# A two-layer hybrid encoder: layer 0 projects x before its norm is known

## The chip, the cores and the metric

The kernel runs on one core of a Trainium2 chip. The core has a matrix engine (TensorE, PE in the profile, with its weight loads as PEld), a vector engine (VectorE, DVE), a scalar engine (ScalarE, ACT), a general engine (GpSimd, POOL) and SyncE (SP), which here only issues loads. The metric is the device time of one execution in microseconds (us).

## What is computed

Two layers over 256 tokens of width 2048, all in float32. A layer norms its input, projects it to seven groups of columns, runs a convolution group and an attention group, joins them in an output projection, and adds a normed embedding times a gate. The reference, cut to what matters:

```python
for i in range(DEPTH):                      # DEPTH = 2
    hn = _rmsnorm(h, norm_g[i])
    u = hn @ w_in[i]
    a_val, a_glu, a_z, q, k, v, b_z = jnp.split(u, offs, axis=-1)
    ya = _conformer_conv(a_val, a_glu, ...) * jax.nn.silu(a_z)
    yb = _window_attention(q, k, v, bias_band, sink[i]) * jax.nn.silu(b_z)
    h = h + jnp.concatenate([ya, yb], axis=-1) @ w_out[i]
    e = _rmsnorm(p[i] @ w_pe[i], pe_g[i])
    h = h + e * jax.nn.sigmoid(h @ w_pg[i])
return _rmsnorm(h, final_g)
```

`_rmsnorm(x, g)` is x times g, divided by the root of the mean square of the token's 2048 values.

## The kernel before

Everything is kept transposed: channels lie on the 128 partitions, the 256 tokens along the row. A float32 product is made of three fast ones (`mm3`, lines 398 to 403): weights and operand are each split into a rounded part and the rest (hi and lo), and hi x hi, hi x lo and lo x hi are summed in a PSUM bank.

Weights come as a stream of half tiles of 128 x 1024 values, two to a load of 1 MB (`load`, line 158, into one of three `raw` buffers, issued by SP). `split` (line 163) makes hi on ACT (a cast) and lo on DVE (a subtraction) into one of five `w` buffers; `ahead` and `get` keep it four halves ahead of use. One half tile feeds 24 matmuls, a step. After each step `pump` (line 203) issues some taps of the convolution on DVE (`conv`, line 557, 3.3, 2.6 or 3.3 taps a step by stage) and one piece of each side generator (`embed`, `attention`, `lnorm`). For PE, DVE and ACT the order of the program is the order of execution; the DMA queues run theirs in order too.

The order of a layer: embedding e = p @ w_pe (eight pairs of tiles), convolution tiles `ag` (value and gate, 8), k, v, then pairs of zb and q with the attention behind them, za, the output projection o in two halves (first the attention's part, then the convolution's), and the gate g.

Layer 0 starts so: loads of p, the first weights and x on two queues (lines 281 to 296). The embedding's matmuls run in plain float32, since its weights needn't be split then. Meanwhile ACT squares x, DVE sums the squares into `hacc`, and PE sums over the partitions (`rstd_col`, line 349); POOL takes the power -0.5, PE transposes the root into a row (`rstd_row`, line 364). Only then `operand` (line 447) makes x times gain times root, split into `hg`, and the `ag` matmuls start. The first two `ag` tiles run together (line 584). `glu` (line 573) evicts a tile: ACT takes the sigmoid of the gate from PSUM into `u`, DVE multiplies it with the value into `a` (a part of the tile az).

`embed` (line 521) issues the squares of e between the convolution's steps: ACT squares, POOL adds into `eacc`; later come the root and the scaling of e. `bias_prep` (line 326) makes the attention's bias by one matmul `fps`. In the attention, q is evicted into `qq` (line 691): for each half ACT scales it, DVE makes the rest; the scores `sc` (line 636) follow two steps later.

## Time and profile before

| what | us |
|---|---|
| median of 3 runs | 937.8 |
| lowest of them | 936.86 |
| the profiled execution | 938.7 |
| its span, from first to last instruction | 936.9 |

The mean granted clock of PE was 0.996. In the profile a row of the timeline reads: start, duration, engine, line of the code, operation, what it writes and reads, shape, count, and in brackets how long the engine was idle before it and what ended that. A row of the windows reads: the stretch, its length, then busy time and count for PE, PEld, DVE, ACT and POOL (only those that a filter leaves), the granted clock, the busy share of the DMA engines and GB/s. A row of groups ends in count, total and mean ns of one.

### The profile page before, as it was taken

The numbers are of one execution on the slowest core, as the hardware profiler recorded it, in microseconds if no ns is written. First come the engines' busy times: TensorE is split into PE (matmuls) and PEld (weight loads), VectorE is DVE, ScalarE is ACT, GpSimd is POOL, SyncE is SP. The second block draws the span as 40 slices with busy tenths as digits, with TensorE's granted clock in tenths as the row PEclk, the third lists the DMA queues.
The fourth block names the chain that finished last, engine by engine and source line by source line (L and its number), as shares of the span: only waits on it lengthen the run. The fifth ranks groups of instructions, "written<-read, shape, count | busy, mean of one in ns | idle before, by whom it ended". The sixth has DMA issues, their size and how long they took to land.

```text
span 936.9 us, 19106 instructions
## 1 busy us (share of the span) xinstructions
PE 923.9 (99%) x7960; PEld 909.7 (97%) x7960; DVE 767.6 (82%) x1282; ACT 549.2 (59%) x830; POOL 82.0 (9%) x79
## 2 busy tenths in 40 slices
PE   8999999999999999999999999999999999999995
PEld 7999999999999999999999999999999999999995
DVE  3999999998887786787679999999888877777663
ACT  4655454878874555554566445568788546445551
POOL 0013001001000000011102100100100000000111
PEclk9999999999999999999999999999999999999999
DMA  7674656555547455546555556565555554654532
GB/s 298 226 250 150 220 180 230 190 196 175 189 171 247 166 209 212 191 181 230 211 189 193 181 212 226 174 213 196 183 169 180 193 197 152 247 183 179 200 114 91
DMA packets 29011, 182.55 MB, mean 195 GB/s; under 512 B 3595, under 2 KB 4156, under 8 KB 9084
## 3 DMA queue, kind: packets, MB, share of 16 engines
q1 hardware_dynamic: 24284, 165.70, 50.1%
q0 software_dynamic: 3344, 12.88, 4.2%
q10 hardware_dynamic: 1296, 2.75, 0.8%
q8 instruction: 62, 1.02, 0.4%
q14 instruction: 25, 0.20, 0.1%
HBM read 177.09 MB, written 4.23 MB: 194 GB/s over the span
## 4 chain that ended last, share of the span: by engine, by line
PE 75%; DVE 19%; ACT 2%; issue 2%; DMA 1%; ACTq 0%; DVEq 0%
DVE cz L566 8%; DVE w L171 8%; PE o L401 6%; PE o L402 6%; PE o L403 6%; PE g L401 6%; PE g L403 6%; PE g L402 6%; PE ag L403 4%; PE ag L401 4%; PE ag L402 4%; PE za L401 3%; PE za L403 3%; PE za L402 3%; PE av L679 2%
## 5 line engine op out<-in xcount | busy, mean ns | idle before, releaser
L171 DVE TENSOR_TENSOR w<-raw,w 128x1024 fp32r<-128x1024 f32 x306 | 375.1, 1234 | 99.5 <-ACT w L168 98.6
L168 ACT CAST w<-raw 128x1024 fp32r<-128x1024 f32 x308 | 315.6, 1046 | 157.8 <-PE ag L403 42.5
L566 DVE SCALAR_TENSOR_TENSOR cz<-az,pars,cz 128x241 f32<-128x241 f32 (+11 forms) x480 | 215.9, 499 | 1.0
L401 PE MATMUL ag<-hg,w 128*128 128x256 f32 x512 | 141.8, 277 | 0.0
L403 PE MATMUL ag<-hg,w 128*128 128x256 f32 x512 | 141.6, 277 | 0.0
L402 PE MATMUL ag<-hg,w 128*128 128x256 f32 x512 | 141.5, 276 | 0.0
L403 PE MATMUL g<-h,w 128*128 128x256 f32 x512 | 141.3, 276 | 0.0
L401 PE MATMUL g<-h,w 128*128 128x256 f32 x512 | 141.3, 276 | 0.0
L402 PE MATMUL g<-h,w 128*128 128x256 f32 x512 | 141.3, 276 | 0.0
L401 PEld LDWEIGHTS ag<-hg,w 128*128 128x128 f32 x512 | 96.1, 188 | 0.9 <-ACT u L575 0.8
L403 PEld LDWEIGHTS ag<-hg,w 128*128 128x128 f32 x512 | 96.2, 188 | 0.1
L402 PEld LDWEIGHTS ag<-hg,w 128*128 128x128 f32 x512 | 96.1, 188 | 0.0
L401 PEld LDWEIGHTS g<-h,w 128*128 128x128 f32 x512 | 96.1, 188 | 0.0
L402 PEld LDWEIGHTS g<-h,w 128*128 128x128 f32 x512 | 96.1, 188 | 0.0
L403 PEld LDWEIGHTS g<-h,w 128*128 128x128 f32 x512 | 96.1, 188 | 0.0
L401 PE MATMUL za<-hg,w 128*128 128x256 f32 x256 | 71.7, 280 | 0.0
L401 PE MATMUL o<-yb,w 128*128 128x256 f32 x256 | 71.6, 280 | 0.0
L401 PE MATMUL q<-hg,w 128*128 128x256 f32 x256 | 71.5, 279 | 0.0
L401 PE MATMUL zb<-hg,w 128*128 128x256 f32 x256 | 71.5, 279 | 0.0
L402 PE MATMUL o<-yb,w 128*128 128x256 f32 x256 | 71.0, 277 | 0.0
L402 PE MATMUL q<-hg,w 128*128 128x256 f32 x256 | 71.0, 277 | 0.0
L403 PE MATMUL zb<-hg,w 128*128 128x256 f32 x256 | 71.0, 277 | 0.0
(223 smaller groups left out, 2264.4 us busy)
## 6 DMA issues: line engine op xcount, KB each, us to landing
raw<-in_wst SPq DMA_DIRECT2D x153, 1024.0 KB, 4.9
bias<-fscr POOLq DMA_DIRECT2D x16, 384.0 KB, 3.9
raw<-in_wst SPq DMA_DIRECT2D x4, 512.0 KB, 7.9
az<-in_xT POOLq DMA_DIRECT2D x4, 512.0 KB, 6.0
hscr<-e POOLq DMA_DIRECT2D x2, 1024.0 KB, 5.6
az<-hscr POOLq DMA_DIRECT2D x4, 512.0 KB, 5.4
x<-in_xT SPq DMA_DIRECT2D x3, 512.0 KB, 8.2
out_t<-og ACTq DMA_DIRECT2D x4, 256.0 KB, 3.0
```

The source lines that it names most:

```text
L168: nc.scalar.copy(hi, raw)
L171: nc.vector.tensor_sub(lo, raw, hi.bitcast(F32))
L401: nc.tensor.matmul(o, w[:, 0], x[:, 0], start=start, stop=False, skip_group_check=True)
L402: nc.tensor.matmul(o, w[:, 0], x[:, 1], start=False, stop=False, skip_group_check=True)
L403: nc.tensor.matmul(o, w[:, 1], x[:, 0], start=False, stop=stop, skip_group_check=True)
L566: nc.vector.scalar_tensor_tensor(acc[:, t, lo_:hi_], a[:, t, lo_ + s:hi_ + s], w(k), acc[:, t, lo_:hi_], ALU.mult, ALU.add)
L679: nc.tensor.matmul(o[hh * HD:(hh + 1) * HD, x, :], v[:, kt, g * HD:(g + 1) * HD], pt[hh][:, kt, :], start=x == 0 and kt == 0, stop=kt == 1 ...
```

## The change

In layer 0 the operand is x times gain alone, so that no matmul of the projection waits for the norm; the root multiplies the results. As the factor belongs to a token, which lies along the row, DVE multiplies each result by a row of roots (`evicted`), and v, with tokens on partitions, is scaled by a column in ACT's copy. The root is taken from a second copy of x with tokens on partitions (`xtok`): ACT squares eight pieces and accumulates each piece's sum, DVE adds them, POOL takes the power, PE transposes.

The first two `ag` tiles are loaded in pieces and multiplied in four groups of four k-slices each, as the pieces land. The embedding of layer 0 comes behind them, in three products. x by tokens, p and the constants are loaded later. In both layers the squares of e move to the second half of the output projection, with DVE in place of POOL for the sums, and the root's row there gets two more small matmuls (`settle`). Layer 0 issues 3.2 taps a step in the first stage, and one warming matmul is added.

```diff
-NWARM = 6
-QQ = ((4, 5), (2, 4))
+NWARM = 7
+QQ = (2, 4)
...
-    for q in range(4):
-        out.append(("w_pe", q, 0, 2))
+    if l:
+        out += W_PE
     for ts in FIRST_TILES:
         for k0 in (0, 8):
             for t in ts:
                 for off in (OFF_VAL, OFF_GLU):
                     out.append(("w_in", off + tile_cols(t), k0, 8))
+        if l == 0 and len(ts) == 2:
+            out += W_PE
...
+        raw = raws[h // 2][:, h % 2, c] if h // 2 in raws else alone[h][:, c]
+        hi, lo = spl[h][:, 0, c], spl[h][:, 1, c]
         nc.scalar.copy(hi, raw)
-        spl[h] = w
-        if h not in (4, 5):
-            nc.vector.tensor_sub(lo, raw, hi.bitcast(F32))
-    def first_lo(h):
-        w = spl[h]
-        nc.vector.tensor_sub(w[:, 1], raws[h // 2][:, h % 2, :], w[:, 0].bitcast(F32))
+        nc.vector.tensor_sub(lo, raw, hi.bitcast(F32))
...
-    RATES = (3.3, 2.6, 3.3)
+    RATES = ((3.2, 2.6, 3.3), (3.3, 2.6, 3.3))
...
-    load_half(0, 0, nc.scalar, 2)
-    pf = load_p(0)
-    load_half(0, 1)
-    load_x(0, nc.scalar)
...
+    load_x(0, 1)
+    load_part(0, 0, nc.scalar, 4)
+    nc.sync.dma_start(gains, gain)
+    load_x(1, 1)
+    load_part(0, 1, nc.scalar, 4)
+    load_x(2, 2)
+    load_part(1, 0, nc.scalar)
+    load_part(2, 0, nc.scalar)
+    load_part(3, 0)
     load_x(4)
-    load_half(1, 0, nc.scalar)
+    for x in range(4):
+        load_part(x, 1)
     load_x(8)
+    for x in range(4, 8):
+        load_part(x, 0)
     load_x(12)
-    load_half(1, 1)
-    load_half(2, 0)
-    nc.sync.dma_start(gains, gain)
-    load_half(2, 1)
+    for x in range(4, 8):
+        load_part(x, 1)
...
+    def small_loads():
+        for t in (pf[:, 0, 0:1], xts[0][:, 0:1]):
+            nc.vector.memset(t, 0.0)
+        nc.sync.dma_start(pf, pT[0])
+        for x, y in enumerate(xts):
+            nc.sync.dma_start(y, xtok[x // 4, :, x % 4 * 2 * S:(x % 4 + 1) * 2 * S])
+    def later_loads():
+        for t in (pars[:, 0:1], oh[:, 0:1], sinkt[:, 0:1]):
+            nc.vector.memset(t, 0.0)
+        nc.sync.dma_start(pars, par)
...
-                if l == 0 and j // 2 < 4:
-                    for k in (4 * (j // 2), 4 * (j // 2) + 2):
-                        if k < KT - 2:
-                            square_acc(hacc, h[k // 8][:, k % 8:k % 8 + 2, :], k == 0, nc.vector)
-                    if j // 2 == 3:
-                        sq = wk.tile([P, 2, S], F32, name="sq", tag="sq", bufs=3)
-                        nc.scalar.activation(sq, h[1][:, 6:8, :], AF.Square)
-                        hparts = halves_of(sq) + [fold(hacc)]
-                if j // 2 == QQ[l][0]:
-                    dg = rstd_col(hparts, D, f"rh{l}")
-                    ahead(5 if l == 0 else Cursor.h - 1 - q + 5)
-                if j // 2 == QQ[l][1]:
-                    rbs.append(rstd_row(dg, f"rh{l}", copy=False))
-                    if l == 0:
-                        first_lo(4)
-                        operands(0, 1)
-                        first_lo(5)
-                        subs.pop(0)()
-                        operands(2, 1)
...
+            for n in range(4):
+                c = slice((n % 2) * (HALF // 2), (n % 2 + 1) * (HALF // 2))
+                ks = range(4 * n, 4 * n + 4)
+                for y in range(4):
+                    for k in ks[2 * y:2 * y + 2]:
+                        i, kk = k // 8, k % 8
+                        hi, lo = (x[:, kk, :] for x in halves(hg[i]))
+                        nc.scalar.activation(hi, h[i][:, kk, :], AF.Copy, scale=gcol(l, k))
+                        nc.vector.scalar_tensor_tensor(lo, h[i][:, kk, :], gcol(l, k), hi.bitcast(F32),
+                                                       ALU.mult, ALU.subtract)
+                    if n == 0 and y == 0:
+                        split_part(0, slice(0, HALF // 4))
+                        split_part(0, slice(HALF // 4, HALF // 2))
+                    else:
+                        split_part(4 * (n // 2) + y, c)
+                if n == 1:
+                    small_loads()
+                for y in range(4):
+                    w = spl[4 * (n // 2) + y].rearrange("p t (k c) -> p t k c", k=8)
+                    for k in ks:
+                        mm3(firsts[y // 2][:, y % 2, :], w[:, :, k % 8, :], hg[k // 8][:, :, k % 8, :],
+                            y % 2 == 0 and k == 0, k == KT - 1)
+            for y in range(8):
+                spl.pop(y)
+            Cursor.h = 8
+            pp = wk.tile([P, 4 * S + 32], F32R, name="pp", tag="qq")
+            pp = pp[:, 24:24 + 4 * S].rearrange("p (x k s) -> p x k s", x=2, k=2)
+            hilo(pp[:, 0], pp[:, 1], pf)
+            ahead(8)
+            later_loads()
+            xs = wk.tile([P, 2, 4], F32, name="xs", tag="xs", bufs=1)
+            for x, y in enumerate(xts):
+                nc.scalar.activation(y, y, AF.Square, accum_out=xs[:, x // 4, x % 4:x % 4 + 1])
+            nc.vector.tensor_add(xs[:, :, 0:2], xs[:, :, 0:2], xs[:, :, 2:4])
+            nc.vector.tensor_add(xs[:, :, 0], xs[:, :, 0], xs[:, :, 1])
+            rcol = root(xs[:, :, 0], D, f"rh{l}")
+            ahead(9)
+            scaled = rstd_row(rcol, f"rh{l}", settle=2)
...
+        def evicted(b, scale=None, scaled=scaled):
+            if scaled is None:
+                return b
+            u = wk.tile([P, 2, S], F32, name="ev", tag="sq", bufs=3)
+            if scale is None:
+                nc.vector.tensor_mul(u, b, bcast2(scaled))
             else:
+                nc.vector.scalar_tensor_tensor(u, b, scale, bcast2(scaled), ALU.mult, ALU.mult)
+            return u
...
+            b = evicted(b)
...
+            for q in range(4):
+                n = Cursor.h
+                Cursor.h += 1
+                w = get(n).rearrange("p t (j k c) -> p t j k c", j=4, k=2)
+                if q < 2:
+                    glu(q, firsts[q])
+                for jj in range(0, 4, 2):
+                    copied(4 * q + jj, epair(w, jj, pp))
+                pump()
...
+            while Cursor.h % NHALF < O_LAST:
+                yield
+            for j in range(0, KT, 2):
+                square_acc(eacc, e[j // 8][:, j % 8:j % 8 + 2, :], j == 0, nc.vector)
+                yield
+            es = fold(eacc)
+            yield
+            dg = rstd_col([es], D, f"re{l}")
+            yield from wait(2)
+            eb = rstd_row(dg, f"re{l}", "reb", settle=2)
+            while not state["enorm"]:
...
-        b = pair(hg, f"k{l}")
+        b = evicted(pair(hg, f"k{l}"))
...
+                nc.scalar.activation(v[:, b, :], vb[b][:, 0, :], AF.Copy, scale=rcol[:, b:b + 1])
...
-            b = pair(hg, f"zb{l}_{i}")
+            b = evicted(pair(hg, f"zb{l}_{i}"))
             nc.scalar.activation(zb[:, i:i + 2, :], b, AF.Silu)
             b = pair(hg, f"q{l}_{i}")
+            qs = -(HD ** -0.5)
+            if l == 0:
+                b, qs = evicted(b, qs), 1.0
...
-            b = pair(hg, f"za{l}_{t}")
+            b = evicted(pair(hg, f"za{l}_{t}"))
...
+        "xtok": np.ascontiguousarray(x[0].reshape(2, P, D)),```

On PE, at the start of the program: ahead of the first `ag` matmul stand, before, the embedding (e), the column of the root (rh0c) and its row (rh0b).

```order
L261 MATMUL warm<-zeros 128x256 x6
L487 MATMUL e<-p_90,raw_87 128x256 x16
L487 MATMUL e<-p_90,raw_95 128x256 x4
L354 MATMUL rh0c<-ones,sq 128x1 x4
L354 MATMUL rh0c<-ones,fold 128x1 x2
L487 MATMUL e<-p_90,raw_95 128x256 x4
L368 MATMUL rh0b<-ident,rh0col 128x128 x2
L487 MATMUL e<-p_90,raw_95 128x256 x8
L401 MATMUL ag_0_260<-hg_0_214,w_196 128x256
```

Now the 192 matmuls of the two tiles come right behind the warming ones; after the last of them stand the row of the root and the embedding, whose weights are w_441 (half 8).

```order
L447 MATMUL ag_1_154<-hg_1_152,w_317 128x256
L448 MATMUL ag_1_154<-hg_1_152,w_317 128x256
L413 MATMUL rh0b<-ident,rh0col 128x128 x2
L415 MATMUL rh0b<-ones 128x1 x2
L446 MATMUL e<-pp,w_441 128x256
L447 MATMUL e<-pp,w_441 128x256
```

The root's row moved from ahead of the first tiles to between them and the embedding.

On ACT, the same place before: eight squares of x, then the casts of the first two weights.

```order
L388 ACTIVATE hacc<-x 128x512
L391 ACTIVATE sq<-x 128x512 x6
L495 ACTIVATE sq<-x 128x512
L168 CAST w_196<-raw_100 128x1024
L168 CAST w_198<-raw_100 128x1024
L470 COPY e_131<-e 128x512 x5
```

Now the operand (hg) and the halves of the first tiles come first; at their end stand p's cast, the cast of half 8 (from raw_435, which is raw4) and then the eight squares of x by tokens.

```order
L560 ACTIVATE hg_1_152<-x,gains 128x256 x2
L178 CAST w_311<-raw_110 128x512
L178 CAST w_314<-raw6alone 128x512
L178 CAST w_317<-raw7alone 128x512
L480 CAST pp<-p_90 128x512
L178 CAST w_441<-raw_435 128x1024
L585 ACTIVATE xt,xs<-xt 128x512 x8
L178 CAST w_466<-raw_435 128x1024
L419 COPY rh0rb<-rh0b 128x256
```

The squares moved behind the casts of the first tiles and behind that of half 8.

On SP's queue, which issues these loads, before: p, the first weights and x, then the constants, then the stream (raw_192 is its first whole load).

```order
L265 DMA p_90<-in_pT 128x512
L274 DMA raw_87<-in_wst 128x1024
L277 DMA x<-in_xT 128x1024 x3
L274 DMA raw_95<-in_wst 128x1024
L274 DMA raw_100<-in_wst 128x1024
L292 DMA gains<-in_gain 128x48
```

Now, from the last quarter of the first tiles' loads on:

```order
L285 DMA x<-in_xT 128x1024
L282 DMA raw_110<-in_wst 128x512 x2
L282 DMA raw6alone<-in_wst 128x512
L282 DMA raw7alone<-in_wst 128x512
L346 DMA p_90<-in_pT 128x512
L348 DMA xt<-in_xtok 128x512 x8
L165 DMA raw_435<-in_wst 128x2048
L165 DMA raw_437<-in_wst 128x2048
```

p, which stood first, and the eight pieces of x by tokens (xt) now stand between the first tiles' weights and raw4 (raw_435).

More of the change, by code (lines that the diff above doesn't have):

```diff
@@ L129, in trunk_kernel @@
 @with_exitstack
-def trunk_kernel(ctx: ExitStack, tc: tile.TileContext, xT, pT, wst, par, gain, relb, sinkp, onehot, out):
+def trunk_kernel(ctx: ExitStack, tc: tile.TileContext, xT, xtok, pT, wst, par, gain, relb, sinkp, onehot, out):
     nc = tc.nc
@@ L293, in trunk_kernel @@
-    load_half(2, 1)
-    state["raw"] = 2
-    pars = cst.tile([P, DEPTH * PW], F32, name="pars")
-    nc.sync.dma_start(pars, par)
+    for x in range(4, 8):
+        load_part(x, 1)
+    xts = []
+    for b in range(2):
+        for c in range(4):
+            if b == 0:
+                y = wk.tile([P, 2, S], F32, name="xt", tag="s", bufs=4)
+            elif c < 2:
+                y = wk.tile([P, 2, S], F32, name="xt", tag="ptt", bufs=2)
+            else:
+                y = wk.tile([P, 2, 3 * P], F32, name="xt", tag="bias", bufs=2)
+            y = y.rearrange("p a b -> p (a b)")[:, 0:2 * S]
+            xts.append(y)
@@ L439, in trunk_kernel @@
     for l in range(DEPTH):
-        e = halves(bigt(f"e{l}"))
-        eacc = wk.tile([P, 2, S], F32, name="eacc", tag="hacc")
+        if l:
+            e = halves(bigt(f"e{l}"))
+            eacc = wk.tile([P, 2, S], F32, name="eacc", tag="hacc")
         hg = []
@@ L577, in glu, with embed @@
             conv_q.append(conv(t))
-        for ts in FIRST_TILES:
+        if l == 0:
+            e = halves(bigt(f"e{l}"))
+            eacc = wk.tile([P, 2, S], F32, name="eacc", tag="hacc")
+            for q in range(4):
+                n = Cursor.h
+                Cursor.h += 1
+                w = get(n).rearrange("p t (j k c) -> p t j k c", j=4, k=2)
+                if q < 2:
+                    glu(q, firsts[q])
+                for jj in range(0, 4, 2):
+                    copied(4 * q + jj, epair(w, jj, pp))
+                pump()
+        def embed(l=l, eacc=eacc, e=e):
+            if l == 0:
+                yield from wait(4)
+                bias_prep()
+            while Cursor.h % NHALF < O_LAST:
[9 more added lines that the diff above has]
+            while not state["enorm"]:
+                yield
+            for j in range(KT):
+                d = e[j // 8][:, j % 8, :]
+                nc.vector.scalar_tensor_tensor(d, d, pcol(l, PO_PE + j), eb, ALU.mult, ALU.mult)
+                yield
+        state["enorm"] = False
+        engen = embed()
+        side.append(engen)
+        for ts in FIRST_TILES[l == 0:]:
             bs = [bank(f"ag{l}_{t}") for t in ts]
```

163 lines of the change are left out of this document (80 added, 83 removed).

## The prediction

> **What bounds the kernel now.** I read the page's shares first, then the pace of the matmuls by windows, then the start by timeline. "Step" is one half weight tile: 24 matmuls.
>
> ```profile
> PE 923.9 (99%) x7960; PEld 909.7 (97%) x7960; DVE 767.6 (82%) x1282; ACT 549.2 (59%) x830; POOL 82.0 (9%) x79
> ```
>
> TensorE (PE) is busy all the time. Its pace, from the windows of the gate tiles g and of the first projection tiles ag, and the end of the second ag tile:
>
> ```profile
> 382.10:469.10 87.00, 87.00 (x768) 87.00 (x768) 4.58 (x8) 1.00 0.58 206
> ...
> 24.66:48.50 23.84, 22.93 (x192) 22.58 (x193) 0.40 (x1) 0.38 (x1) 1.00 0.66 230
> ...
> 48.73 0.38 ACT L575 ACTIVATE u<-ag 128x256 f32<-128x256 f32 x1 [3.85 <-PE ag L403]
> ...
> 42.08 0.96 PE fps L329 x2
> ```
>
> 768 matmuls in 87.0 us are 113.3 ns each, 2.72 us a step: that is the bound wherever PE is fed. The two first tiles (192 matmuls, 21.8 us at that pace) end at 48.5 us, after 0.96 us of the bias matmul, which the change moves behind a later tile. So the mark to beat is 48.5 - 1.0 = 47.5 us: embedding and first two tiles done. Only what shifts this mark, or makes PE wait later, counts. How that start goes now:
>
> ```profile
> 16.35 1.05 PE L354 MATMUL rh0c<-ones,sq 128*128 128x1 f32 x8 [1.15 <-ACT sq L495]
> 17.71 3.31 PE L487 MATMUL e<-p,raw 128*128 128x256 f32 x8
> 21.24 3.79 PE L487 MATMUL e<-p,raw 128*128 128x256 f32 x16
> 24.69 0.47 PE L401 MATMUL ag<-hg,w 128*128 128x256 f32 x1
> ```
>
> The embedding's matmuls lie over the wait for x, its squares and its root; the first ag matmul starts at 24.69.
>
> **The change, part by part: the first tiles.** The norm leaves the operand, so ag can start once a quarter of its loads is there. Warming matmuls run to about 6 us, then 192 x 113.3 ns: the two tiles end near 28 to 29 us, if PE is fed. Loads needed for them are 6.3 MB (x 2.10, eight weight halves 4.19):
>
> ```profile
> 0.00:6.00 6.00, 4.81 (x14) 3.79 (x15) 0.49 (x4) 1.28 (x1) 0.70 (x6) 1.00 0.55 183
> 6.00:20.00 14.00, 12.39 (x59) 10.20 (x58) 5.89 (x9) 7.93 (x13) 1.63 (x1) 0.94 1.04 404
> 930.00:934.00 4.00, 0.00 (x0) 0.00 (x0) 1.43 (x3) 0.00 (x0) 0.85 (x1) 0.87 1.03 380
> ```
>
> The last column is GB/s. 1.1 MB by 6 us, the other 5.2 MB at 380 to 404 take 13 to 14 us: all there by 20 us, PE decides. That alone would gain much.
>
> **The root.** But the transposes of the root now stand on PE between the first tiles and the embedding, and the root is ready late. On SP's queue behind the 6.3 MB come p (0.26 MB) and x by tokens (2.10 MB), and only then raw4, the 1 MB with the embedding's weights. ACT's order is the cast of w8, which needs raw4, and behind it the eight squares. So raw4 holds back the root. It is the 9.72nd MB: 8.62 MB after 6 us. At 404 (rows of 4 KB mostly) it is there at 27.4, at 380 (the output's 2 KB rows, the length that most of the new loads have) at 28.7. I take 28.5 with the landing, since the new loads are nearer to the second row; ends 27.4 and 29.5.
> By the Trainium skill's page "DMA: Bandwidth & Descriptors" (section Specifications) pieces from 512 B run at line rate, while one core's HBM limit is about 358 GB/s; by the first raw4 lands at 27.4, by the second at 30.1. The rows of 404 and 380 pass the second figure, and 380 against 404 is slower than the first rule has it.
>
> From there, with these rows:
>
> ```profile
> 11.10 1.13 ACT L391 ACTIVATE sq<-x 128x512 f32<-128x512 f32 x2
> ...
> 16.53 1.04 ACT L168 CAST w<-raw 128x1024 fp32r<-128x1024 f32 x1 [0.24 <-DMA raw<-in_wst]
> ...
> 171.71 0.49 ACT L649 ACTIVATE s<-s,nm 128x256 f32<-128x256 f32 x1
> ...
> 172.20 0.49 ACT L649 ACTIVATE s<-s,nm 128x256 f32<-128x256 f32 x1
> ...
> 177.86 1.31 ACT L657 ACTIVATE s<-s,den 128x256 f32<-128x256 f32 x3 [0.69 <-DVE den L654]
> ...
> 17.88 0.16 DVE L359 TENSOR_SCALAR rh0v<-rh0c 128x2 f32<-128x2 f32 x1 [1.00 <-PE rh0c L354]
> ...
> 18.13 1.63 POOL L361 TENSOR_TENSOR rh0col<-rh0v,mhalf 128x2 f32<-128x2 f32 x1 [16.81 <-DVE rh0v L359]
> ...
> 926.46 0.70 POOL L361 TENSOR_TENSOR rfcol<-rfv,mhalf 128x2 f32<-128x2 f32 x1 [9.41 <-DVE rfv L359]
> ...
> 313.42 0.38 PE L368 MATMUL rv0b<-ident,rv0col 128*128 128x128 f32 x2
> 313.63 0.50 PE L370 MATMUL rv0b<-ones 128*128 128x1 f32 x4
> 314.00 0.36 PE L401 MATMUL o<-yb,w 128*128 128x256 f32 x1
> ```
>
> Cast 1.04: 29.5. Squares follow 0.50 us apart without an accumulator (1.13 - 0.63); the exponentials with one stand 0.49 apart, the plain ones 0.41 ((1.31 - 0.49)/2), so it adds about 0.1: 8 x 0.6 = 4.9, 34.4. Three small DVE steps of 0.16: 34.9. POOL's power 1.63 as at the start now (0.70 at the end of the kernel is the other bound), and 0.1 for hand-overs: 36.6. Transposes and the two settling matmuls 0.6 (313.42 to 314.00): the embedding starts at 37.2. Its 96 matmuls (32 in three products) take 10.9: 48.1. PE has then idled 8 us, and a clock drop is to be paid:
>
> ```profile
> 18.00:19.00 1.00, 1.00 (x4) 0.59 1.14 369
> 19.00:20.00 1.00, 1.00 (x4) 0.50 0.98 410
> 20.00:21.00 1.00, 1.00 (x4) 0.50 0.52 213
> 21.00:22.00 1.00, 1.00 (x6) 0.70 0.08 16
> ```
>
> The third figure from the right is the granted clock: after the weak stretch from 15 to 18 us it lacks 0.41 + 0.50 + 0.50 + 0.30 = 1.7 us of work. I take the same 1.7 (ends 0 and 2): 49.8. **Start: 49.8 - 47.5 = +2.3**; ends -1.4 (raw4 at 27.4, power 0.70, no clock loss) and +3.6 (29.5, clock loss 2).
>
> **The norm behind the projection.** DVE now scales 21 tiles (8 ag, 1 k, 4 zb, 4 q, 4 za) out of PSUM, by the row of the output's addition:
>
> ```profile
> L768 DVE TENSOR_TENSOR az<-o,az 128x512 f32<-128x512 f32 x16 | 10.9, 684 | 0.7 <-PE o L403 0.6
> ...
> 81.20:113.80 32.60, 32.60 (x290) 32.60 (x289) 32.53 (x53) 16.03 (x20) 5.95 (x4) 1.00 0.55 187
> ...
> 135.90:157.80 21.90, 21.90 (x194) 21.90 (x194) 21.80 (x39) 11.32 (x13) 4.21 (x4) 1.00 0.59 201
> ...
> 338.60:360.00 21.40, 21.40 (x191) 21.40 (x190) 16.48 (x19) 10.52 (x12) 0.00 (x0) 1.00 0.68 246
> ```
>
> DVE (the third busy time) is full from 81 to 158 us. 21 x 0.68 = 14.4 us more there, plus some 0.5 us a tile of waiting for the sigmoid. Against it stands what leaves: the embedding's seven additions on POOL go to DVE in the second half of the output projection, where it is idle a fifth (16.48 of 21.40). On POOL each stops DVE's taps:
>
> ```profile
> 63.91 1.63 DVE L566 SCALAR_TENSOR_TENSOR cz<-az,pars,cz 128x246 f32<-128x246 f32 x4
> 65.47 1.21 DVE L171 TENSOR_TENSOR w<-raw,w 128x1024 fp32r<-128x1024 f32 x1
> 66.60 2.29 DVE L566 SCALAR_TENSOR_TENSOR cz<-az,pars,cz 128x248 f32<-128x248 f32 x3
> ...
> 66.78 1.44 POOL L392 TENSOR_TENSOR eacc<-eacc,sq 128x512 f32<-128x512 f32 x1 [3.88 <-ACT sq L391]
> ...
> L576 DVE TENSOR_TENSOR az<-ag,u 128x256 f32<-128x256 f32 x16 | 6.6, 414 | 1.2 <-ACT u L575 1.2
> ```
>
> Three taps took 2.29 beside an addition, four 1.63 alone: 1.0 us each, 7 us returned. In ag that balances. A tile takes DVE four splits of 1.13 (65.47 to 66.60), 12.8 taps of 0.39 (four in 1.56), the product's 0.4, the scaling's 0.68 and the 0.5: 11.1 against PE's 10.88. So it falls back some 1.5 us over the tiles, and its splits run up to four steps ahead: cost there 0. The first scores have no such cover:
>
> ```profile
> 158.00 0.59 ACT L695 ACTIVATE qq<-q 64x512 fp32r<-64x512 f32 x1 [1.67 <-PE q L403]
> ...
> 162.00 0.69 DVE L696 SCALAR_TENSOR_TENSOR qq<-q,qq 64x512 fp32r<-64x512 f32 x1
> 163.35 0.69 DVE L696 SCALAR_TENSOR_TENSOR qq<-q,qq 64x512 fp32r<-64x512 f32 x1 [0.66 <-ACT qq L695]
> ...
> 164.09 0.39 PE L636 MATMUL sc<-keys0h,qq 128*128 128x256 f32 x1 [0.23 <-DVE qq L696]
> ```
>
> DVE reaches q 4 us late and PE already waits 0.23. Added ahead of it: scaling k 0.7 with 0.5 of waiting, scaling zb 0.7, scaling q 0.7; ACT's first part, done early now, follows that scaling, 0.6. Sum 3.2; a fold and the removed dependence of the second ACT part give back 1. So PE waits some 2 us, and 1 us more at the next pairs: **+3** (ends 0 and +6). Two settling pairs in the embedding's row of both layers, 0.37 each: +0.7. Layer 1 loses its POOL additions too, worth at most the few tenths that its scores wait: -0.3. Loads, copies of e and later taps are covered by PE's 2.72 us steps.
>
> **Sum:** 2.3 + 3.0 + 0.7 - 0.3 = +5.7. The profiled execution took 938.7 (span 936.9), 0.9 over the median 937.8; I set the change on the median: 943.5.
>
> **Rivals.** (1) *The root is hidden*, faster: the embedding follows the first tiles at 28.8 + 0.6, ends at 40.3, the mark falls by 7.2, and with 3.4 for the rest the kernel takes 934, or 931 if the scores do not wait. It decides if the root is ready by 29, so raw4 landed by 20; the bytes speak against it. (2) *Even*: root quicker, clock kept, scores uncharged: -1.4 + 0.4, 937. (3) *DVE becomes the bound*, slower: if POOL's relief does not come, 14.4 + 4 us are added where DVE is full, less the 5 us that it may lag: 13 on top of 2.3, 953. Full windows speak for it, the quick taps without POOL against it.
>
> **Chances.** Forecast 0.58 (939 to 949), rival 1 0.13, rival 2 0.16, rival 3 0.10, the rest beyond. Eight in ten reach from 935.5 to 949.5. Two per cent is 18.8 us, about what a measurement can tell from no change; no case but a worse third passes it. Faster 0.01, same 0.96, slower 0.03.
>
> **What would show it.** First ag matmul near 6 to 7 us and its 192nd near 29; a PE gap of about 8 us ended by POOL; raw4 at 28.5 just ahead of ACT's cast of w8; granted clock of half in the first embedding matmuls; third tile from 49.8; sc waiting 2 us on DVE's qq. Wrong if the gap is missing, if DVE's tile in ag takes over 10.9, or if sc does not wait.

## The result: 27 us slower

| | median, us | lowest to highest | ratio to before, 95% interval |
|---|---|---|---|
| before | 937.3 | 936.3 to 937.9, and one run of 2,849 (without it the median is 936.9) | |
| changed | 964.7 | 961.3 to 965.5 | 1.0289, 1.0270 to 1.0308 |

The forecast was 943.5 in a range of 935.5 to 949.5, with 0.96 on "within two per cent". The kernel became slower by 2.9 per cent.

### The profile page after: what moved, and what is told of

Its sections match the earlier page's. It is cut to its first block, busy times and chain, and to the rows that moved or that the text cites. A ratio compares the mean times of both kernels' runs of the same rounds, so it can differ in the third digit from the quotient of the medians.

```text
span 963.1 us, 19287 instructions
## 1 busy us (share of the span) xinstructions
PE 936.3 (97%) x7994; PEld 922.5 (96%) x7994; DVE 773.2 (80%) x1323; ACT 554.9 (58%) x862; POOL 57.6 (6%) x65
## 4 chain that ended last, share of the span: by engine, by line
PE 82%; DVE 11%; ACT 2%; DMA 2%; issue 2%; SPq 0%; POOL 0%; DVEq 0%; ACTq 0%
PE g L446 6%; PE g L448 6%; PE g L447 6%; PE o L446 6%; PE o L447 6%; PE o L448 6%; PE ag L446 5%; PE ag L447 5%; PE ag L448 5%; DVE w L179 5%; DVE cz L621 4%; PE za L446 3%; PE za L447 3%; PE za L448 3%; PE q L446 2%; PE q L447 2%
## 5 line engine op out<-in xcount | busy, mean ns | idle before, releaser
L179 DVE TENSOR_TENSOR w<-raw,w 128x1024 fp32r<-128x1024 f32 (+2 forms) x317 | 378.2, 1202 | 123.8 <-ACT w L178 123.2
L178 ACT CAST w<-raw 128x1024 fp32r<-128x1024 f32 (+2 forms) x317 | 316.6, 1025 | 133.9 <-PE g L448 28.9
L621 DVE SCALAR_TENSOR_TENSOR cz<-az,pars,cz 128x241 f32<-128x241 f32 (+13 forms) x480 | 204.9, 477 | 1.9 <-ACT cz L614 1.0
L446 PE MATMUL g<-h,w 128*128 128x256 f32 x512 | 142.6, 278 | 0.0
L447 PE MATMUL g<-h,w 128*128 128x256 f32 x512 | 142.6, 278 | 0.0
L448 PE MATMUL g<-h,w 128*128 128x256 f32 x512 | 142.6, 278 | 0.0
L446 PE MATMUL ag<-hg,w 128*128 128x256 f32 x512 | 141.6, 277 | 0.6 <-ACT w L178 0.6
L448 PE MATMUL ag<-hg,w 128*128 128x256 f32 x512 | 141.6, 276 | 0.1
L447 PE MATMUL ag<-hg,w 128*128 128x256 f32 x512 | 141.5, 276 | 0.1
L446 PEld LDWEIGHTS ag<-hg,w 128*128 128x128 f32 x512 | 96.1, 188 | 1.9 <-ACT w L178 1.0
L448 PEld LDWEIGHTS g<-h,w 128*128 128x128 f32 x512 | 97.2, 190 | 0.0
L448 PEld LDWEIGHTS ag<-hg,w 128*128 128x128 f32 x512 | 96.1, 188 | 0.5 <-DVE w L179 0.5
L447 PEld LDWEIGHTS ag<-hg,w 128*128 128x128 f32 x512 | 96.1, 188 | 0.3 <-DVE hg L561 0.3
L446 PEld LDWEIGHTS g<-h,w 128*128 128x128 f32 x512 | 96.1, 188 | 0.0
L447 PEld LDWEIGHTS g<-h,w 128*128 128x128 f32 x512 | 96.1, 188 | 0.0
L446 PE MATMUL zb<-hg,w 128*128 128x256 f32 x256 | 72.3, 283 | 0.8 <-ACT w L178 0.8
L448 PE MATMUL zb<-hg,w 128*128 128x256 f32 x256 | 72.0, 281 | 0.9 <-DVE w L179 0.8
L446 PE MATMUL o<-ya,w 128*128 128x256 f32 x256 | 72.3, 282 | 0.0
L448 PE MATMUL o<-ya,w 128*128 128x256 f32 x256 | 72.0, 281 | 0.0
L447 PE MATMUL o<-ya,w 128*128 128x256 f32 x256 | 72.0, 281 | 0.0
L446 PE MATMUL o<-yb,w 128*128 128x256 f32 x256 | 71.9, 281 | 0.0
L447 PE MATMUL zb<-hg,w 128*128 128x256 f32 x256 | 71.9, 281 | 0.0
```

What stands on the lines that cost most here:

```text
L178: nc.scalar.copy(hi, raw)
L179: nc.vector.tensor_sub(lo, raw, hi.bitcast(F32))
L446: nc.tensor.matmul(o, w[:, 0], x[:, 0], start=start, stop=False, skip_group_check=True)
L447: nc.tensor.matmul(o, w[:, 0], x[:, 1], start=False, stop=False, skip_group_check=True)
L448: nc.tensor.matmul(o, w[:, 1], x[:, 0], start=False, stop=stop, skip_group_check=True)
L621: nc.vector.scalar_tensor_tensor(acc[:, t, lo_:hi_], a[:, t, lo_ + s:hi_ + s], w(k), acc[:, t, lo_:hi_], ALU.mult, ALU.add)
```

## The profile after the change

The profiled execution took 964.9 us, its span 963.1; the 26.2 us more of span are what is looked for below. The first row is the page's busy time and shares, the second the span with the mean granted clock (before: 0.996).

```profile
PE 936.3 (97%) x7994; PEld 922.5 (96%) x7994; DVE 773.2 (80%) x1323; ACT 554.9 (58%) x862; POOL 57.6 (6%) x65
...
core 0: 963.1 us, clock 0.987
```

PE's busy time grew by 12.4 us with 34 matmuls more, and its idle time by about as much again. So only about half of the loss can be waits; most of the other half is in matmuls that take longer. The waits, from the view of who waited for whom (total in us, times, longest):

```profile
PE rh0b L413 <- POOL rh0col L406: 7.6, 1, 7.6
PE sc L736 <- DVE qq L799: 4.4, 2, 4.2
PE re1c L395 <- DVE fold L424: 1.9, 1, 1.9
...
PE zb L446 <- ACT w L178: 0.8, 1, 0.8
PE zb L448 <- DVE w L179: 0.8, 1, 0.8
```

Where the time went, by the first matmul of each stage on PE's timeline:

| stage, us | before | changed | more |
|---|---|---|---|
| start to the first matmul of k | 113.8 | 119.2 | 5.4 |
| from there to the first scores | 49.6 | 55.8 | 6.2 |
| first scores to the output projection, layer 0 | 129.8 | 132.2 | 2.4 |
| output projection, layer 0 | 89.0 | 93.2 | 4.2 |
| gate of layer 0 to the output projection of layer 1 | 364.9 | 364.8 | -0.1 |
| output projection, layer 1 | 89.4 | 94.6 | 5.2 |
| gate of layer 1 and end | 100.5 | 103.3 | 2.8 |

**The start.** Rows of the timeline: ACT's cast of the embedding's first weights (L178), the first of the eight squares (L585), the power on POOL, and PE's transposes and first embedding matmul. The columns are start, duration, engine, instruction, and the idle time before it with its releaser.

```profile
30.69 1.04 ACT L178 CAST w<-raw 128x1024 fp32r<-128x1024 f32 x1 [6.99 <-DMA raw<-in_wst]
31.64 0.63 ACT L585 ACTIVATE xt<-xt 128x512 f32<-128x512 f32 x1
...
37.32 0.70 POOL L406 TENSOR_TENSOR rh0col<-rh0v,mhalf 128x2 f32<-128x2 f32 x1 [36.01 <-DVE rh0v L404]
...
38.08 0.69 PE L413 MATMUL rh0b<-ident,rh0col 128*128 128x128 f32 x2 [7.57 <-POOL rh0col L406]
...
39.27 0.56 PE L446 MATMUL e<-pp,w 128*128 128x256 f32 x1
```

ACT stood idle for 7 us for raw4 with the squares behind it. The embedding began at 39.3, and the first matmul of the third tile followed at 52.7.

**The clock.** Windows of 2 us behind the three long waits (busy time and count by engine, then granted clock, DMA share, GB/s):

```profile
38.00:40.00 2.00, 1.92 (x9) 1.92 (x10) 0.83 (x1) 0.55 (x2) 0.03 (x1) 0.50 0.31 45
40.00:42.00 2.00, 2.00 (x12) 2.00 (x11) 1.20 (x2) 2.00 (x3) 0.00 (x0) 0.50 0.70 266
42.00:44.00 2.00, 2.00 (x13) 2.00 (x13) 2.00 (x3) 1.94 (x2) 0.00 (x0) 0.62 0.53 221
174.00:176.00 2.00, 0.97 (x3) 0.85 (x4) 1.45 (x3) 1.95 (x4) 0.00 (x0) 0.50 0.93 393
176.00:178.00 2.00, 2.00 (x11) 2.00 (x11) 2.00 (x4) 1.78 (x2) 0.00 (x0) 0.50 0.01 4
178.00:180.00 2.00, 2.00 (x11) 2.00 (x11) 2.00 (x4) 0.00 (x0) 0.00 (x0) 0.50 0.00 0
838.00:840.00 2.00, 2.00 (x14) 2.00 (x14) 0.54 (x1) 2.00 (x3) 0.00 (x0) 0.71 0.68 250
840.00:842.00 2.00, 2.00 (x11) 2.00 (x10) 2.00 (x4) 0.37 (x1) 1.06 (x1) 0.50 0.57 238
842.00:844.00 2.00, 2.00 (x18) 2.00 (x18) 1.12 (x2) 0.84 (x2) 0.00 (x0) 0.94 0.25 49
```

Eleven or twelve matmuls in a window that holds 18 else. What half the clock lacks, counted from the moment PE works again, is 0.96 + 1.0 + 0.76 = 2.7 us at the start, 0.5 + 1.0 + 1.0 = 2.5 behind the scores, and 0.6 + 1.0 + 0.1 = 1.7 in layer 1's output projection.

**The DVE queue.** Waits of DVE from the end of the first tiles to the first scores, two rows of before and four of the changed kernel:

```profile
DVE w L171 <- ACT w L168: 0.9, 2, 0.5
DVE qq L696 <- ACT qq L695: 0.7, 1, 0.7
...
DVE w L179 <- ACT w L178: 6.3, 10, 1.6
DVE az L632 <- ACT u L631: 2.9, 6, 0.5
DVE keys0l L698 <- ACT keys0h L696: 0.9, 2, 0.5
DVE qq L799 <- ACT qq L798: 0.7, 1, 0.7
```

Some 2 us of waiting before, 10.8 after. How one such wait comes about (timelines of DVE and ACT; zb's tile is scaled, then the next split waits):

```profile
161.71 0.68 DVE L598 TENSOR_TENSOR ev<-zb,rh0rb 128x512 f32<-128x512 f32 x1
162.42 0.63 ACT L788 ACTIVATE az<-ev 128x512 f32<-128x512 f32 x1 [6.72 <-DVE ev L598]
162.96 1.04 ACT L178 CAST w<-raw 128x1024 fp32r<-128x1024 f32 x1
164.03 1.23 DVE L179 TENSOR_TENSOR w<-raw,w 128x1024 fp32r<-128x1024 f32 x1 [1.64 <-ACT w L178]
...
172.81 0.69 DVE L600 SCALAR_TENSOR_TENSOR ev<-q,rh0rb 128x512 f32<-128x512 f32 x1
```

ACT's silu of zb waits for DVE's scaling, ACT's next cast stands behind the silu, and DVE's split waits for that cast. PE had finished q at 165.0; DVE came to it at 172.8, 7.8 us late instead of 4.0.

**The pace.** Matmuls in a window: before, in the first tiles and a little later; and those of the changed kernel's last gate (the prediction's row for the same gate tiles of layer 0 had 768 in 87.0 us):

```profile
32.00:42.00 10.00, 10.00 (x86) 1.00 0.59 211
50.00:60.00 10.00, 10.00 (x91) 1.00 0.87 309
...
859.70:951.00 91.30, 90.62 (x768) 1.00 0.39 139
```

With PE fed, the granted clock at 1.00 and the same instructions, 768 matmuls take 90.6 us here, 118 ns each. Starts of successive matmuls show two paces, 113.3 and 117.7 ns, and next to nothing between; a pace holds for as long as only large matmuls follow one another. Added up over all groups of 18 successive starts whose mean distance lies between 115.5 and 119.5 ns, the excess over 113.3 is 3.8 us before and 10.5 after: **some 6.7 us of the loss**, 3.4 of it in the last gate and 2.1 in layer 0's output projection. With the groups cut at other places the same count gives 5.5 to 7.1.

## The experiments

The times are medians; "changed" is 964.7. Waits, marks and paces are those of the one profiled execution of each kernel; "three together" and "last version" are combinations that are told further below. The marks of the kernels that tell most, first matmul of the stage in us:

| | before | changed | squares first | consumers later | three together | last version |
|---|---|---|---|---|---|---|
| third tile (embedding and first two tiles done) | 48.5 | 52.7 | 45.0 | 52.4 | 42.6 | 42.6 |
| first scores | 163.4 | 175.0 | 169.6 | 168.9 | 159.9 | 159.9 |
| output projection, layer 0 | 293.1 | 307.2 | 301.8 | 298.6 | 294.2 | 290.2 |
| its gate | 382.1 | 400.4 | 395.1 | 392.0 | 388.2 | 380.6 |
| output projection, layer 1 | 747.0 | 765.2 | 759.9 | 756.8 | 752.9 | 745.8 |
| last gate | 836.4 | 859.8 | 853.3 | 851.8 | 843.6 | 834.7 |
| slow pace, us in all | 3.8 | 10.5 | 11.6 | 12.0 | 11.7 | 3.5 |

**Squares first.** The DMA issues stay; the cast of w8 goes behind the root.

```
-            ahead(8)
+            while state["raw"] < 6:
+                state["raw"] += 1
+                load(state["raw"])
             later_loads()
...
             rcol = root(xs[:, :, 0], D, f"rh{l}")
+            ahead(8)
             ahead(9)
```

> The squares of x by tokens stand on ACT ahead of the cast of the embedding's first weights; DMA order unchanged. Theory (the root hangs on raw4 through ACT's order): the squares run from about 24 us while the first tiles compute, the root is ready by 30.5, PE then waits only for raw4's cast and split, 2.5 us instead of 7.6; the embedding starts at 33 to 34 instead of 39.3, and the kernel takes 957 to 959 instead of 964.7. Rival (raw4's landing alone is the bound, the order of ACT does not matter): embedding starts at 38 or later, 963 to 965. Second rival (DVE is the bound up to the first scores, so an earlier start is given back there): embedding earlier, but the wait of sc grows by as much, 962 to 965.

958.5 us. POOL's power and the third embedding matmul, from the timeline:

```profile
30.12 0.70 POOL L406 TENSOR_TENSOR rh0col<-rh0v,mhalf 128x2 f32<-128x2 f32 x1 [28.81 <-DVE rh0v L404]
...
33.62 0.38 PE L448 MATMUL e<-pp,w 128*128 128x256 f32 x1 [0.76 <-DVE w L179]
```

The root is ready when the first tiles end, and no half clock follows there: the embedding is done 7.7 us earlier. ACT's order was the gate. Of the 7.7 us, 5.5 are left at the first scores: PE now waits 2.9 us instead of 1.6 for zb's first weights, with half the clock for 3.4 us behind it (from 138.3). Part of the gain is given back to ACT and DVE.

**No scaling after the first two tiles.** `evicted` returns the tile as it is. This kernel leaves out a step of the norm and so computes other values.

```
-            if scaled is None:
+            if scaled is None or Cursor.h > 12:
...
-            if l == 0:
-                b, qs = evicted(b, qs), 1.0
```

> Leaves out the scaling by the root for every tile after the first two (six ag, k, four zb, four q, four za); the root's own work and the first two tiles keep it. Theory (the scalings and the waits they bring on ACT and DVE cost the first scores): the waits of 4.4 us on qq and 1.6 us on the first zb weights vanish, the clock loss of some 2.9 us behind the scores too, 955 to 957 instead of 964.7; DVE's waits between 53 and 178 us fall from 10.8 to about 2. Rival (the loss there comes from the late start and the moved additions, not from the scalings): 962 to 965.

954.2 us. PE no longer waits for qq or for zb's weights, and no half clock follows: the first scores come 6.0 us earlier. DVE's waits did not fall as expected (9.2 us in all, 4.7 of them on casts), but it came to q 1.8 us after PE instead of 7.8.

In the profiled execution (951.3, the fastest of the four) the last gate ran at 113 ns, other than in the changed kernel:

```profile
849.40:936.60 87.20, 87.05 (x768) 1.00 0.42 146
```

The instructions of layer 1 are those of the changed kernel. In both, a block of two transposes and two settling matmuls stands 888 large matmuls ahead of the gate's end. Here the stretch ahead of that block ran at 118 ns and the one behind it at 113; in the changed kernel it was the other way round. So the same block doesn't always leave the same pace: in these two it turned the pace over.

**Consumers one step later.** The scalings stay.

```
-            nc.scalar.activation(u, b[:, 1, :], AF.Sigmoid)
-            nc.vector.tensor_mul(a[:, t, :], b[:, 0, :], u)
-            conv_q.append(conv(t))
+            def gated(t=t, b=b, l=l, a=a, conv=conv):
...
+                later(gated)
...
+                later(split_keys)
...
+                later(silu)
...
+                later(split_q)
```

> All scalings stay; what ACT and DVE do with a scaled tile in layer 0 (sigmoid and product, parts of the keys, silu, parts of q) is issued one step later, behind the next cast and split. Theory (idle time from ACT and DVE waiting on each other in order, 10.8 us on DVE between 53 and 178, puts DVE behind, not the 0.68 us of a scaling): DVE's waits there fall to 2 to 4 us, sc waits under 1 us instead of 4.4, no clock loss behind it, 956 to 959. Rival (the busy time of the scalings is what counts): DVE's waits fall but sc still waits 3 us or more, 962 to 966. Third way (the parts of q issued a step later are themselves late): sc waits more than 4.4, over 965.

957.2 us. The waits in the changed place, PE's and DVE's:

```profile
PE sc L750 <- DVE qq L819: 0.3, 2, 0.2
...
DVE az L634 <- ACT u L633: 1.6, 2, 1.1
DVE w L179 <- ACT w L178: 1.4, 4, 0.7
```

The same 6.1 us at the first scores as without any scaling. So not the scalings' busy time but the order in which ACT and DVE waited for one another made the scores late. The start, where PE still waited 7.8 us, and the fold are as before.

**A step between fold and root.**

```
             es = fold(eacc)
-            yield
+            yield from wait(2)
             dg = rstd_col([es], D, f"re{l}")
```

> The sums over e behind the output projection: PE's root matmuls come one step later after the fold, in both layers. Theory (PE waits 1.9 us for the fold in layer 1, and the clock falls for it): no wait there, no half clock at 839 to 843, 960 to 961 instead of 964.7 (1.9 of wait and 2.2 of clock); the slow pace of 118 ns in the last gate tiles may stay or go, worth another 3.9. Rival (the wait only shows another bound, DVE behind PE in the whole output projection): the wait reappears a step later, 963 to 965.

961.6 us, at the slow end of what was expected. PE's wait for the fold and the half clock behind it are gone; layer 1's output projection takes 90.7 us instead of 94.6. The last gate stays at 118 ns.

**The sums over e where they were,** in both layers.

```
-            while Cursor.h % NHALF < O_LAST:
-                yield
             for j in range(0, KT, 2):
-                square_acc(eacc, e[j // 8][:, j % 8:j % 8 + 2, :], j == 0, nc.vector)
-                yield
+                yield from wait(2)
+                square_acc(eacc, e[j // 8][:, j % 8:j % 8 + 2, :], j == 0)
+            yield from wait(12 + 8 * l)
             es = fold(eacc)
-            yield
+            yield from wait(3)
             dg = rstd_col([es], D, f"re{l}")
-            yield from wait(2)
-            eb = rstd_row(dg, f"re{l}", "reb", settle=2)
+            yield from wait(10)
+            eb = rstd_row(dg, f"re{l}", "reb")
+            yield from wait(50)
```

> The sums of squares of e and their root go back to where they stood before, in both layers: under the first projections and scores, with the additions on POOL, and without settling matmuls. Theory (the additions on POOL slow DVE by 1 us each, the work behind the output projection costs 4.2 us in layer 0 and 8.6 us in layer 1): the output projections and the last gate tiles take what they took before (89.1, 89.6 and 87.2 us), 12 to 13 us back, but sc waits 10 to 12 us instead of 4.4; 958 to 962. Rival (POOL's additions do not slow DVE where it waits for ACT anyway): sc waits under 6 us, 951 to 954. Other rival (the slow pace of matmuls does not hang on these root matmuls): the last gate tiles stay at 90.5 us, 962 to 965.

966.8 us, a miss. The first scores came at 183.1, 8.0 later than in the changed kernel: the relief that the prediction counted for DVE (7 us) fits that. But only 6.0 us came back behind instead of 12: the last gate still took 90.5, and every matmul from 785 on, 1,414 of them, went at 118 ns, with layer 1's code doing the same steps in the same order as before. The slow pace does not need the root of e in its new place.

**No settling matmuls** behind the root of e.

```
-            eb = rstd_row(dg, f"re{l}", "reb", settle=2)
+            eb = rstd_row(dg, f"re{l}", "reb", settle=0)
```

> The two settling matmuls behind each root of e are left out; they change no value. Theory (the pace of 113 or 118 ns is drawn anew by each small group of matmuls, so another group draws another pace): the last 768 matmuls take 87.0 us in some executions and 90.5 in others, whatever the settling; 960 to 965, and PE's waits as in the changed kernel. Rival (the settling pair causes the slow pace): last gate tiles at 87.0 us in all executions, 960 to 961. Other rival (the pair is what prevents it elsewhere): layer 0's gate tiles become slow too, 966 to 969.

964.8 us; the last gate again at 118 ns. The pair neither causes nor prevents it there.

This trace also limits what can be said of the clock. PE waited the same 1.93 us for the fold, but the clock stayed full behind it (a row of PE's timeline and a window of PE alone, whose last four figures are matmuls, granted clock, DMA share and GB/s):

```profile
838.46 0.58 PE L395 MATMUL re1c<-ones,fold 128*128 128x1 f32 x4 [1.93 <-DVE fold L424]
838.40:842.40 4.00, 3.94 (x34) 1.00 0.72 262
```

Six of the traces have this wait of 1.93 us. Half the clock followed in three (changed, no scaling, consumers later) and not in the other three (squares first, no settling matmuls, embedding ahead of the root).

**The embedding ahead of the root.** raw4 and raw5 are loaded ahead of x by tokens, their halves are split ahead of the squares, and the transposes follow three quarters of the embedding. The first two tiles are evicted behind the transposes.

```
         nc.sync.dma_start(pf, pT[0])
+        while state["raw"] < 5:
+            state["raw"] += 1
+            load(state["raw"])
         for x, y in enumerate(xts):
...
+                if q == 3:
+                    scaled = rstd_row(rcol, f"rh{l}", settle=2)
+                    glu(0, firsts[0])
```

> The embedding's two weight chunks are loaded ahead of x by tokens, PE computes three quarters of the embedding behind the first tiles and only then the root's transposes. Theory (the start's loss is the order of the loads and of the root's transposes): no PE wait over 1 us between 8 and 45 us, no half clock, embedding done at 42 to 43 instead of 52.9; the first scores still wait on DVE, part of the gain is given back there as with the squares alone (5.5 of 7.7 kept); 954 to 957. Rival (DVE is the bound up to the first scores): the wait of sc and zb grows by the gain, 961 to 965.

961.0 us, a miss, and the rival's time. The start did as expected (done at 42.7, full clock, no wait of over 1 us from 8 us on), but sc then waits 5.3 us and the mean of the second norm 3.5 us for DVE, both with half the clock. With DVE as late as it is, an earlier start is worth 3.7 of 10.1 us.

**These three together:** the last start, the later consumers, the step behind the fold.

> The last start, the consumers of scaled tiles one step later, and PE's root of e one step later after the fold, together. Theory (the three losses are separate and add up): 10 for the start, 7.6 and 3.1 for the others, 943 to 946. Rival (an earlier start only finds DVE later): 949 to 953. If the last gate tiles draw the fast pace as well, up to 4 less.

948.7 us, 2.7 over the upper bound and just under the rival's 949. Up to the first scores everything added up (3.5 us ahead of the kernel before). Then one long wait was left, of PE for taps at the end of the attention:

```profile
PE mean L855 <- DVE cz L624: 3.2, 2, 1.7
```

**Small groups.** Between half tiles of the gate, groups of n small matmuls of 128 columns (layer 0) or one (layer 1), in a bank of their own.

```
+        def small(n, c):
+            t = bank("probe")
+            for x in range(n):
+                nc.tensor.matmul(t[:, 0, 0:c], ones, ident[:, 0:c], start=True, stop=True, skip_group_check=True)
+        probes = [(n, 1 if l else P) for n in (1, 1, 2, 2, 3, 3, 1, 1, 4, 4, 2, 2)]
...
+                    small(*probes.pop(0))
                     step(b[:, x, :], h1, x == 0, False)
                     step(b[:, x, :], h1, False, True)
```

> The three changes together, with twelve extra small groups of matmuls between the half tiles of the gate in each layer: 1, 1, 2, 2, 3, 3, 1, 1, 4, 4, 2, 2 matmuls, 128 columns wide in layer 0 and 1 column wide in layer 1, in a bank nobody reads. They change no value. Theory (each small group draws the pace of the matmuls behind it anew, 113 or 118 ns, and it stays until the next): the pace changes at some of the 24 groups and nowhere else, both paces occur in both layers; if the number of matmuls in the group decides, equal groups do the same. Rival (the pace hangs on something outside PE's instructions, such as the loads or the other engines): the groups change nothing, layer 1's gate is slow throughout and layer 0's fast, or the pace changes between groups.

961.9 us in its one execution; the 24 groups themselves take most of the 13 us more. The groups on PE's timeline, from the third on in layer 0 and the first in layer 1; the profile counts each small matmul twice, so x4 is a pair:

```profile
411.68 0.60 PE L966 MATMUL probe<-ident,ones 128*128 128x128 f32 x4
417.79 0.61 PE L966 MATMUL probe<-ident,ones 128*128 128x128 f32 x4
423.70 0.83 PE L966 MATMUL probe<-ident,ones 128*128 128x128 f32 x6
429.82 0.83 PE L966 MATMUL probe<-ident,ones 128*128 128x128 f32 x6
435.95 0.38 PE L966 MATMUL probe<-ident,ones 128*128 128x128 f32 x2
441.63 0.38 PE L966 MATMUL probe<-ident,ones 128*128 128x128 f32 x2
447.31 1.05 PE L966 MATMUL probe<-ident,ones 128*128 128x128 f32 x8
453.86 1.05 PE L966 MATMUL probe<-ident,ones 128*128 128x128 f32 x8
460.22 0.60 PE L966 MATMUL probe<-ident,ones 128*128 128x128 f32 x4
...
863.33 0.28 PE L966 MATMUL probe<-ident,ones 128*128 128x1 f32 x2
869.00 0.28 PE L966 MATMUL probe<-ident,ones 128*128 128x1 f32 x2
874.66 0.50 PE L966 MATMUL probe<-ident,ones 128*128 128x1 f32 x4
880.76 0.50 PE L966 MATMUL probe<-ident,ones 128*128 128x1 f32 x4
886.86 0.72 PE L966 MATMUL probe<-ident,ones 128*128 128x1 f32 x6
```

From one group's start to the next lie the group and 48 large matmuls. Behind the first pair that takes 6.11 us, behind the second 5.91: 0.20 less, which is 48 times 4.2 ns. Behind the two triples 6.12 and 6.13, behind the two of four 6.55 and 6.36. In layer 0 each of the six groups of even number turned the pace over, and none of the six of odd number touched it. In layer 1 a lone matmul left 113 ns each time, also where 118 had been (at 863); pairs and fours left 118; one triple left it slow, one fast. The pace changed at groups and nowhere else in the gates. So here it hung on the small matmuls that went before; nothing points to loads or other engines.

**Taps sooner**, on the three together; za's silu goes a step later with `later`, and layer 1's sums over e stand as before.

```
-    RATES = ((3.2, 2.6, 3.3), (3.3, 2.6, 3.3))
+    RATES = ((3.2, 2.6, 3.8), (3.3, 2.6, 3.3))
```

> On the three changes together: layer 0's convolution taps go at 3.8 a step instead of 3.3 in the attention, the silu of za one step later, and layer 1's sums over e go back to where they stood before. Theory (the wait for the mean of 3.2 us and the clock behind it come from taps left over at the end; layer 1's root of e costs 1.3 us where it was moved to): no wait of mean over 0.5 us, the half clock at 293 gone, layer 1 as before; 942 to 945 instead of 948.7. Rival (DVE is the bound there, taps taken earlier make sc or the weights late): PE waits of 2 us or more between 150 and 280 us, 946 to 950. The slow pace may add or take up to 4.

945.6 us, just over the expected range. The mean no longer waits and layer 1's root of e is back where it was, but the slow pace now takes 14.5 us in all: everything from 764 to the end of the gate runs at 118 ns.

**A lone matmul of one column** a step behind the blocks that are followed by long stretches; on the version of 945.6 us, and on the changed kernel alone.

```
+    def nudge():
+        t = bank("nudge")
+        nc.tensor.matmul(t[:, 0, 0:1], ones, ident[:, 0:1], start=True, stop=True)
```

> The last version with one single matmul of one column, in a bank nobody reads, a step after each of the blocks behind which the pace can stay slow for long: before the first silu tile, behind the root of the second norm, behind layer 0's root of e, and in the first step of the gate. It changes no value. Theory (a lone matmul brings back 113 ns, as at 863 us with the small groups, and does not disturb it where it holds): slow stretches of over 20 us gone, the slow pace costs 5 us or less in all instead of 14.5, last gate tiles 87.0 us; 935 to 938 instead of 945.6, as fast as the kernel before or a little faster. Rival (what a group does depends on where it stands, not on its number): at least one long stretch at 118 ns stays, 939 to 945. Other rival (the lone matmul itself turns 113 into 118 somewhere): over 946.

943.0 us: the rival. The slow pace fell from 14.5 to 8.8; the lone matmul turned slow into fast at 134 and 844 us, but not behind the root of the second norm in either layer.

> The changed kernel as it is, with the same single matmuls at the same places. Theory (6.7 us of its loss are the slow pace behind small groups and have nothing to do with the norm or the loads): the last 768 matmuls take 87.0 us instead of 90.5, the slow pace costs 3 to 5 us in all instead of 10.5, PE's waits stay as they are (7.6, 4.4, 1.9, 1.6); 957 to 960 instead of 964.7. Rival (the slow pace belongs to this order of the work and comes back): 962 to 965.

961.4 us, a smaller gain than expected, between theory and rival. The slow pace fell from 10.5 to 5.4 and the last gate took 87.4 us, but the root of the start waited 9.2 us in this execution and a wait for the fold came up in layer 0 too (1.7).

**A pair instead,** and **one settling matmul instead of two** (and no lone one a step later), both behind the root of the second norm in the version of 943.0.

```
             rb = rstd_row(dg, f"rv{l}", settle=2)
             yield
-            nudge()
+            nudge(2, P)
```

> The last version (943.0 us) with the single matmul behind the root of the second norm replaced by two matmuls of 128 columns, in both layers; no value changes. There the pace was slow before and behind the single one (304 to 365 and 762 to 844 us). Theory (two wide matmuls turn the pace over, as six of six such groups of even number did in layer 0's gate): both stretches at 113 ns from the pair on, the slow pace costs 3 to 4 us in all instead of 8.8, 937 to 939. Rival (the place decides, not the group): one stretch or both stay slow, 940 to 944.

940.5 us, the rival's time. The pair turned the pace over both times: in layer 1 from slow to fast at 773, in layer 0 from fast to slow at 315, since the block ahead had left it fast this time.

```
-            rb = rstd_row(dg, f"rv{l}", settle=2)
+            rb = rstd_row(dg, f"rv{l}", settle=1)
             yield
-            nudge()
```

> The version of 943.0 us with one settling matmul of one column instead of two directly behind the transposes of that root, and none a step later; no value changes. Theory (the number of small matmuls in the block decides, three instead of four here): the pace behind the block is other than in the version before, 113 ns from 311 and from 769 us on, 937 to 939. Rival (one column does not turn the pace over, only wide ones do): slow as before, 942 to 944.

937.0 us, as expected, against 936.7 for the kernel before in the same comparison: ratio 1.0003, interval 0.9994 to 1.0011. With three small matmuls in the block instead of four both stretches are fast, and the slow pace costs 3.5 us in all. Its page:

```profile
PE 922.3 (99%) x7996; PEld 909.4 (97%) x7996; DVE 773.5 (83%) x1316; ACT 556.3 (60%) x862; POOL 72.1 (8%) x72
```

So the whole loss was found and taken back, and no more: the change can be brought level with the kernel before. No version here beats it by more than the measurement can tell.

## Why the prediction was wrong

**The start, +2.3: right mechanism, too small.** The mark moved from 47.5 to 52.7, so +5.2. Step by step: raw4 landed at 30.7, not 28.5 (+2.2); the squares took 5.0 where 4.9 was forecast; the power took 0.70, the lower bound, not 1.63 (-0.9); transposes and settling pair 1.2 instead of 0.6, at half clock (+0.6); the embedding took 13.5 instead of 10.9 and 1.7 for the clock (+0.9). The step that failed is "It is the 9.72nd MB": by 30 us some 10.3 MB had been moved (387 GB/s from 6 to 30 us), and yet raw4 was not there, so part of them must have belonged to the loads issued behind it. By the Trainium skill's page "DMA: Bandwidth & Descriptors", section Specifications, the limit of 358 GB/s had given 30.1, close to the landing, but for another reason than the trace's: the windows of 4 us from 6 to 30 us stand at 360 to 426. The root's wait differed between executions of the kernels with this start, 7.0 to 9.2 us. That raw4 holds back the root through ACT's order was right (squares first: -6.3 us).

**The norm behind the projection, first scores +3: measured 8.6** (6.2 up to the scores and 2.4 behind). The relief was rightly seen: putting POOL's additions back made the scores 8.0 us later. PE lost nothing in ag, as forecast. What failed is the step "11.1 against PE's 10.88": from one scaling to the next (66.66 to 124.93, five tiles) DVE took 11.65 us, so it fell back some 4 us and not 1.5. The waiting was counted only for the sigmoid, and that at its right size (2.9 us in six waits). The rest of the chain ACT, DVE, ACT, DVE was put at nothing: each scaling puts a DVE step ahead of an ACT step that stands ahead of ACT's next cast, on which DVE's next split waits. These waits for casts came to 6.3 us in ten, 3.7 of them before the end of ag; all waits of DVE together 10.8 us instead of 2. (The prediction's sign "if DVE's tile in ag takes over 10.9" was already broken by its own 11.1.) With the consumers a step later and all scalings kept the scores came as early as with no scaling at all. And the wait of PE was given no clock, though the start's was: 2.5 us.

**Two settling pairs, +0.7, and layer 1, -0.3: measured 4.2 + 5.2 in the two output projections.** The move of the sums over e was priced by its settling pairs alone (0.37 us a layer) and not by who would wait there: PE came to the root before DVE's fold in layer 1, 1.9 us and, in this execution, 1.7 of clock. A step between them removed both. Of layer 0's 4.2 us some 2 are the slower pace told next; with the sums put back (the kernel of 966.8 us) that projection took 90.0 us instead of 93.2.

**Not in the sum: 6.7 us of slower matmuls.** The failed sentence is "that is the bound wherever PE is fed". The trace of before shows 118 ns in several of its stretches: 86 matmuls in 10 us where 91 fit from 32 to 42 us, and again at 190 to 209 and 740 to 762. The prediction took its pace from a window that ran at 113, though its own row of the first tiles (24.66 to 48.50) holds a slow stretch. The new small groups, their numbers and the blocks they stand in drew other paces. Which pace follows a block could not have been foretold from before's trace; that there are two, and what a long stretch at the slower costs (4 per cent, 3.4 us for one layer's gate), could.

**What came as told.** The first `ag` matmul at 7.5 and the 192nd at 30.2, a PE gap of 7.6 us that POOL ended, half the clock in the first embedding matmuls, and sc waiting on DVE's qq, 4.4 us instead of 2.

**The rivals.** The third, DVE as the bound, had the sign and named the place, but by a mechanism that did not happen (POOL's relief missing). It was given 953 and 0.10. The clock behind each wait, the fold and the pace make up the way from there to 965.

What stays open: why PE has the two paces, and why a group's number decides the pace behind it. Groups of wide matmuls alone obey odd and even without exception here; narrow ones and blocks of mixed shapes do not.

## What to carry to other kernels

When a step moves from one in-order engine to another, write down the chain of who waits for whom across the next steps of both queues, not only the busy time: here a 0.68 us step cost up to 1.64 us of idle time, and issuing its consumer a step later cured it. Give every new wait of PE of some 2 us or more its clock as well: here the waits of 7.6 and 4.2 us brought 2.7 and 2.5 us more, and one of 1.9 us either 1.7 or nothing. And before a pace from one window is used as the bound, look at it in several: if there are two, read where each begins.

## What was not expected of the hardware

- PE has two steady paces for the same stream of 256-column matmuls at granted clock 1.00, 113.3 and 117.7 ns. Small groups of matmuls can switch between them, and behind a group a pace held for up to 1,404 large matmuls in a row (before, 314 to 473 us).
- A wait of 1.93 us was followed by half the clock, for about 3.4 us, in three of the six traces that have it, beginning 0.6 to 1.5 us after PE had resumed. All fifteen waits of 2.1 us or more in these traces came with half the clock. The Trainium skill's page "TensorE: Matmul & The Clock Gate" (What's actually happening) has the clock fall after an idle window of about 3.4 us; here less than 2 us of idleness could do it, with the drop after the wait was over.
